# Low parts of the first pass's weights: from GpSimd halves to single VectorE operations

## The chip, the cores and the metric

The kernel runs on one core of one Trainium2 chip. That core has a matrix engine (TensorE, PE in the profile; its weight loads are PEld), a vector engine (VectorE, DVE), an activation engine (ScalarE, ACT), a general engine (GpSimd, POOL) and a queue that issues the transfers (SyncE, SP). The metric is the device time of one launch in microseconds (us), lower is better. Times from the profile belong to one profiled execution.

## The reference, cut to what matters

One decoder layer is computed in float32 for a prompt of 2048 rows and for 8 sample rows, with a model width of 1024. Nearly all of the work is products of an activation block with a weight matrix:

```python
h = rmsnorm(x, g_pre)
proj = h @ w_in                      # 1024 x 10248: q,k | v | o | z_a | gates | u | vb | z_b | merge gates
...                                  # conv + SiLU, mLSTM over 128-row chunks, chunk MLP
merged = jax.nn.sigmoid(gate_a) * (y_a @ w_pa) + jax.nn.sigmoid(gate_b) * (y_b @ w_pb)
x = x + rmsnorm(merged @ w_out, g_post)
x = x + jax.nn.sigmoid(x @ w_ple_gate) * rmsnorm(p @ w_ple, g_ple)
```

## The kernel before, in words

**Passes and units.** The prompt is cut into four passes of 512 rows (`p` = 0 to 3; the sample rows ride along in pass 1). In each pass the weights go by as 28 units of 512 columns, in the order of `PASS`: four heads with `v`, `qk`, `og`, `gg` each, then four `ub`, and two each of `pa`, `pb`, `wo` and `wg`. A unit is one block product with seven sub-products instead of eight (a Strassen-Winograd form): its weight is cut into A11, A12, A21, A22 of 512 rows by 256 columns, of which the sums S3 = A11 - A21, S2 = A22 - S3, S1 = A11 + S2 and S4 = A12 - S2 are made, and `ORDER` lists the seven weights that are multiplied: A11, A12, S2, S3, S1, A22, S4. Four passes of 28 units make 784 sub-products, 196 in each pass.

**High and low parts.** Each weight is a tile of 128 partitions by 1024 elements. It is split into a high part in the reduced format float32r (`whi`, a copy on ScalarE) and a low part (`wlo`, the weight minus its high part, made by `sub_hi`, line 129). A sub-product is 24 matmuls: high times high, high weight times low activation, low weight times high activation. So TensorE needs `wlo` in the third matmul of a sub-product.

**The stream of weights.** The class `Stream` prepares the weights some items ahead of the sub-product that runs (`run_unit`): `reach_high` makes the high part two items ahead and issues loads five items ahead (seven after the first pass), `reach_low` makes the low parts of what has a high part, and then, in the first pass, the sums up to three items ahead. In the first pass everything is made from the four loaded blocks; S3 is stored to memory as it is, and S2, S1 and S4 as high and low parts. In passes 1 to 3, S2, S1 and S4 come back already split, and four low parts per unit are made, all on VectorE.

**GpSimd's share.** In the first pass a counter, `uncut`, sends every fourth low part (items 3, 7, 11, ... of the 196, that is 49 of them) to GpSimd, as two subtractions of 128x512. The other 147 are made on VectorE, in one subtraction of 128x1024. As 196 items are seven per unit, the weight that goes to GpSimd changes from unit to unit: S3 in `v`, A11 and S1 in `qk`, A12 and A22 in `og`, S2 and S4 in `gg`, and so on.

**What sets the order.** Each engine works through its own list in order. The lists are fixed when the program is built: the framework's scheduler takes the instructions in the order of the code as priorities and places each on its engine by its own estimate of when operands and buffers are there; waits between engines are semaphores. The weight tiles (raw, sum, high, low) share 13 buffers (`wp`), so a tile that is used longer holds back a later one. GpSimd has other work of its own in all passes: the product of two gates (line 790), the chunk MLP's product (line 1293), the post-norm weight (line 1571), a merge addition (line 139), small copies for the convolution (lines 713 and 720) and the powers of the norms (lines 241 and 242). All transfers are issued from SP's queue.

Of the kernel before, what the change touches and what calls it, by code (L numbers as in the profile page):

```python
# [65 lines left out]
def order(unit):  # L66
    return LATE if unit == ("wo", 0) else ORDER


def width(unit):  # L70
    return 260 if unit == FIRST else 256
# [3 lines left out]
def tile_layer(ctx: ExitStack, tc: tile.TileContext, I, O):  # L75
    nc = tc.nc
    V, S, G, T = nc.vector, nc.scalar, nc.gpsimd, nc.tensor
# [35 lines left out]
    def spill(shape, name):  # L113
        return dp.tile(list(shape), F32, tag=name, name=name)
# [4 lines left out]
    def store(out, in_):  # L119
        nc.sync.dma_start(out=out, in_=in_)  # L120
# [7 lines left out]
    def sub_hi(eng, lo, full, hi):  # L128
        eng.tensor_tensor(lo, full, hi.bitcast(F32), op=ALU.subtract)  # L129
# [126 lines left out]
    class Stream:  # L256
# [4 lines left out]
        def __init__(self):  # L261
            self.items = [(p, u, n) for p in range(NP) for u in PASS for n, *_ in order(u)]
            self.loaded = self.summed = self.split = self.taken = 0
            self.raw, self.high, self.ready, self.kept = {}, {}, {}, {}
            self.uncut = 0

        def tile(self, u, name, dt=F32):
            return wp.tile([P, 4, width(u)], dt, tag="w", name=name)
# [68 lines left out]
        def reach_low(self, n):  # L337
            for key in list(self.high):
                hi = self.high.pop(key)
                lo = self.tile(key[1], "wlo", F32R)  # L340
                pool = key[0] == 0 and self.uncut % 4 == 3
                self.uncut += 1
                for k in ((slice(0, 2), slice(2, 4)) if pool else (slice(0, 4),)):
                    sub_hi(G if pool else V, lo[:, k], self.raw[key][:, k], hi[:, k])
                self.ready[key] = hi, lo
                _, u, name = key
                if name in CUT_KEPT:
                    self.kept[u, name] = [spill([P, 4 * width(u)], f"{name}{x}_{u[0]}{u[1]}") for x in "hl"]
                    for d, t in zip(self.kept[u, name], (hi, lo)):
                        store(d.rearrange("p (k c) -> p k c", k=4), t.bitcast(F32))  # L350
            while self.summed < min(len(self.items), n + self.SUM):
                self.sum(*self.items[self.summed])
                self.summed += 1
# [1406 lines left out]
```

## Time and profile before

| what | value |
|---|---|
| three runs | 2886.32 us median (2886.23 to 2891.51) |
| profiled execution | 2878.66 us, span 2877.0 us |
| granted TensorE clock, mean | 0.973 of full speed |
| PE, DVE, ACT, POOL busy | 94%, 75%, 54%, 18% of the span |
| memory traffic | 267 GB/s over the span |

The span is the time from the first to the last instruction. Busy time is the union of an engine's instructions. "Idle before" is the time that an engine stood still just ahead of a group of instructions, put down to what it waited for last. The first pass lies in the first 797 us: GpSimd's last low part ends at 796.9 us.

### The profile page before, as it was taken

Reading aid. Unit: us, or ns where it says so; the run is one execution under the profiler, and the core shown is the slowest. Engines: PE = TensorE matmul, PEld = TensorE weight load, DVE = VectorE, ACT = ScalarE, POOL = GpSimd, SP = SyncE. Lnnn points to the kernel's source line nnn. Section 1 sums busy time; section 2 is a strip of 40 time slices with the busy share of each in tenths; the row PEclk is TensorE's granted clock in tenths of the full one; section 3 lists DMA queues with packets and bytes.
Section 4 is the critical chain, followed back from the end, with each engine's and each line's share of the span. In section 5 each row is a group of like instructions: output and inputs, shape, how many; then the busy total and the mean of one; then the engine's idle time right before and its main releaser. Section 6 shows DMA issues by size and latency. Waiting matters only on the chain. (4 is left out here: it accounts for less than half of the span.)

```text
span 2877.0 us, 56022 instructions
## 1 busy us (share of the span) xinstructions
PE 2703.2 (94%) x21835; PEld 2639.0 (92%) x21835; DVE 2143.5 (75%) x3513; ACT 1540.1 (54%) x2668; POOL 512.8 (18%) x557
## 2 busy tenths in 40 slices
PE   6999999888899999999999999999999999999998
PEld 6899989888789899989889999999998999999898
DVE  8888888888977667766868766567678766665767
ACT  5555646445645555544456655564356545554445
POOL 3333332334310000101020100101111010101110
PEclk9999999899999999999999999999999999999999
DMA  6567667867777888889878777779878787788886
GB/s 223 220 249 273 242 235 267 295 253 255 262 257 249 287 267 273 276 272 328 285 250 294 254 260 257 253 258 322 311 277 298 241 268 262 252 272 279 317 283 231
DMA packets 268628, 770.37 MB, mean 268 GB/s; under 512 B 30066, under 2 KB 89338, under 8 KB 268355
## 3 DMA queue, kind: packets, MB, share of 16 engines
q1 hardware_dynamic: 268362, 766.79, 77.0%
q8 instruction: 172, 2.82, 0.4%
q14 instruction: 94, 0.76, 0.1%
HBM read 595.29 MB, written 171.53 MB: 267 GB/s over the span
## 5 line engine op out<-in xcount | busy, mean ns | idle before, releaser
L493 PE MATMUL acc<-rhi,whi 128*128 128x256 f32 (+1 forms) x4480 | 1289.6, 288 | 30.9 <-ACT s L124 8.9
L493 PE MATMUL acc<-rhi,wlo 128*128 128x256 f32 (+1 forms) x4480 | 1276.5, 286 | 43.1 <-DVE wlo L129 34.1
L493 PE MATMUL acc<-rlo,whi 128*128 128x256 f32 (+1 forms) x4480 | 1275.2, 285 | 0.0
L493 PEld LDWEIGHTS acc<-rhi,wlo 128*128 128x128 f32 x4480 | 859.3, 192 | 50.3 <-DVE wlo L129 39.6
L493 PEld LDWEIGHTS acc<-rhi,whi 128*128 128x128 f32 x4480 | 860.2, 192 | 41.6 <-ACT s L124 10.3
L493 PEld LDWEIGHTS acc<-rlo,whi 128*128 128x128 f32 x4480 | 859.4, 192 | 0.0
L129 DVE TENSOR_TENSOR wlo<-wraw,whi 128x1024 fp32r<-128x1024 f32 (+1 forms) x462 | 597.7, 1297 | 179.2 <-PE acc L493 77.2
L124 ACT ACTIVATE whi<-wraw 128x1024 fp32r<-128x1024 f32 (+1 forms) x504 | 530.1, 1055 | 349.6 <-PE acc L493 209.4
L490 PE MATMUL acc<-whi,rhi 128*128 128x256 f32 (+1 forms) x1792 | 517.7, 290 | 20.7 <-ACT rhi L124 6.7
L490 PE MATMUL acc<-wlo,rhi 128*128 128x256 f32 (+1 forms) x1792 | 512.0, 287 | 16.2 <-DVE wlo L129 14.1
L490 PE MATMUL acc<-whi,rlo 128*128 128x256 f32 (+1 forms) x1792 | 511.8, 286 | 6.3 <-DVE rlo L129 6.2
L490 PEld LDWEIGHTS acc<-whi,rhi 128*128 128x128 f32 x1792 | 346.1, 193 | 28.0 <-ACT rhi L124 9.6
L490 PEld LDWEIGHTS acc<-wlo,rhi 128*128 128x128 f32 x1792 | 345.1, 193 | 19.8 <-DVE wlo L129 16.9
L490 PEld LDWEIGHTS acc<-whi,rlo 128*128 128x128 f32 x1792 | 346.3, 193 | 8.2 <-DVE rlo L129 8.2
L124 ACT ACTIVATE u<-acc 128x512 f32<-128x512 f32 (+1 forms) x272 | 138.9, 517 | 209.8 <-PE acc L493 156.8
L129 POOL TENSOR_TENSOR wlo<-wraw,whi 128x512 fp32r<-128x512 f32 (+1 forms) x84 | 149.0, 1794 | 291.6 <-ACT whi L124 209.5
L124 ACT ACTIVATE s<-acc 128x512 f32<-128x512 f32 (+1 forms) x136 | 69.4, 513 | 79.3 <-PE acc L493 47.2
L790 POOL TENSOR_TENSOR so<-so,sz 128x512 f32<-128x512 f32 (+1 forms) x32 | 60.2, 1880 | 289.7 <-ACT so L774 171.9
L1293 POOL TENSOR_TENSOR yb<-yb,ub 128x512 f32<-128x512 f32 (+1 forms) x32 | 57.1, 1799 | 293.8 <-DVE ub L1291 127.0
L241 POOL TENSOR_SCALAR aab<-au 128x2 f32<-128x2 f32 x32 | 8.5, 266 | 481.6 <-DVE au L883 481.6
L869 DVE SCALAR_TENSOR_TENSOR cext<-cext,fst,smp 128x258 f32<-128x258 f32 x128 | 60.5, 479 | 36.1 <-PE smp L806 36.0
L720 POOL COPY halo<-raw 128x3 f32<-128x3 f32 x64 | 27.5, 454 | 284.8 <-DVE raw L139 154.7
(365 smaller groups left out, 3899.0 us busy)
## 6 DMA issues: line engine op xcount, KB each, us to landing
wraw<-in_w_main SPq DMA_DIRECT2D x351, 512.0 KB
xh<-xh SPq DMA_DIRECT2D x32, 512.0 KB
sg<-sgm SPq DMA_DIRECT2D x24, 512.0 KB
gsig<-sg SPq DMA_DIRECT2D x24, 512.0 KB
x<-in_x_prompt SPq DMA_DIRECT2D x16, 512.0 KB
ya<-ya SPq DMA_DIRECT2D x32, 256.0 KB
xr<-in_x_prompt SPq DMA_DIRECT2D x32, 256.0 KB
pg<-pg SPq DMA_DIRECT2D x32, 256.0 KB
```

Source lines behind the costliest of these rows:

```text
L124: S.activation(out, in_, AF.Copy)
L129: eng.tensor_tensor(lo, full, hi.bitcast(F32), op=ALU.subtract)
L241: G.tensor_scalar(out, ms, EPS, None, op0=ALU.add)
L490: T.matmul(outs[s], x[:, kt, s * P:(s + 1) * P], wt[:, kt, :], start=first, stop=last, skip_group_check=not opens)
L493: T.matmul(outs[s], wt[:, kt, s * P:(s + 1) * P], x[:, kt, :], start=first, stop=last, skip_group_check=not opens)
L720: G.tensor_copy(halo[:, ct, :], x[:, TP:TP + 3])
L790: G.tensor_tensor(so[:, s], so[:, s], sz[:, s], op=ALU.mult)
L869: V.scalar_tensor_tensor(cext[:, h, kt, :], cext[:, h, kt, :], gt.fst[:, h, self.c:self.c + 1], p3, op0=ALU.mult, op1=ALU.add)
L1293: G.tensor_tensor(y[:, :, l, :], y[:, :, l, :], ub[:, :, l, :], op=ALU.mult)
```

## The change

In the first pass the low part of every weight is now formed on VectorE, in one subtraction over the whole tile, as it was already done for three weights out of four and in the later passes. The counter goes. Nothing else in the code changes: the same operands, the same buffers, the same stores.

```diff
@@ class Stream, __init__
-            self.uncut = 0
@@ class Stream, reach_low
                 hi = self.high.pop(key)
                 lo = self.tile(key[1], "wlo", F32R)
-                pool = key[0] == 0 and self.uncut % 4 == 3
-                self.uncut += 1
-                for k in ((slice(0, 2), slice(2, 4)) if pool else (slice(0, 4),)):
-                    sub_hi(G if pool else V, lo[:, k], self.raw[key][:, k], hi[:, k])
+                sub_hi(V, lo, self.raw[key], hi)
                 self.ready[key] = hi, lo
```

## Rows read from the trace of the kernel before

**Rows 1.** The page: busy time, share of the span and instructions by engine.
```profile
PE 2703.2 (94%) x21835; PEld 2639.0 (92%) x21835; DVE 2143.5 (75%) x3513; ACT 1540.1 (54%) x2668; POOL 512.8 (18%) x557
```

**Rows 2.** Windows: stretch, its length, busy time (instructions) by engine, clock, transfers.
```profile
300.00:400.00 100.00, 93.55 (x752) 91.73 (x751) 86.08 (x128) 58.15 (x93) 34.08 (x34) 0.97 0.69 252
...
500.00:600.00 100.00, 82.68 (x606) 80.66 (x606) 83.30 (x81) 44.74 (x57) 32.97 (x18) 0.86 0.79 282
600.00:700.00 100.00, 83.45 (x617) 80.33 (x616) 93.39 (x97) 49.98 (x77) 44.38 (x19) 0.90 0.68 244
700.00:797.00 97.00, 80.50 (x635) 77.06 (x633) 83.00 (x117) 63.30 (x130) 39.94 (x32) 0.96 0.79 274
797.00:2877.00 2080.00, 2007.25 (x16444) 1963.22 (x16444) 1454.42 (x2604) 1095.82 (x1956) 226.03 (x324) 0.99 0.80 274
```

**Rows 3.** The tile wlo up to 797 us: count, least/median/longest ns.
```profile
L129 DVE TENSOR_TENSOR wlo<-wraw,whi x126: 1187/1218/2348, 16.0 to 788.9; 128x1024 fp32r<-128x1024 f32 x121, 128x1040 fp32r<-128x1040 f32 x5
L129 POOL TENSOR_TENSOR wlo<-wraw,whi x84: 1265/1728/7078, 22.7 to 794.6; 128x512 fp32r<-128x512 f32 x82, 128x520 fp32r<-128x520 f32 x2
...
L129 POOL TENSOR_TENSOR wlo<-wsum,whi x14: 1467/1732/2266, 112.1 to 778.4; 128x512 fp32r<-128x512 f32 x14
```

**Rows 4.** Waits of PE up to 797 us: us in total, times, longest.
```profile
PE acc L493 <- DVE wlo L129: 15.9, 10, 3.8
...
PE acc L493 <- POOL wlo L129: 8.8, 8, 1.9
PE acc L490 <- DVE wlo L129: 7.9, 7, 2.3
...
PE acc L490 <- POOL wlo L129: 2.1, 3, 1.0
```

**Rows 5.** Waits of DVE up to 797 us.
```profile
DVE wraw L136 <- POOL wlo L129: 8.1, 4, 2.4
...
DVE wlo L129 <- ACT whi L124: 2.0, 6, 0.6
```

**Rows 6.** DVE groups up to 797 us: count, busy us, mean ns, idle before.
```profile
L129 DVE TENSOR_TENSOR wlo<-wraw,whi 128x1024 fp32r<-128x1024 f32 x121 | 164.8, 1373 | 2.3 <-ACT whi L124 1.3 <-POOL wlo L129 0.6
L136 DVE TENSOR_TENSOR wraw<-wraw 128x1024 f32<-128x1024 f32 x27 | 40.0, 1482 | 26.3 <-DMA wraw<-in_w_main 22.7 <-DMA gple<-in_g_ple 3.5
...
L718 DVE SCALAR_TENSOR_TENSOR k<-raw,vecs,k 128x512 f32<-128x512 f32 x24 | 24.7, 1047 | 0.0
...
L129 DVE TENSOR_TENSOR cl<-cext,ch 128x516 fp32r<-128x516 f32 x16 | 15.1, 941 | 2.2 <-ACT ch L124 2.2
```

**Rows 7.** The same DVE groups after 797 us.
```profile
L718 DVE SCALAR_TENSOR_TENSOR k<-raw,vecs,k 128x512 f32<-128x512 f32 x72 | 51.2, 747 | 0.2
...
L129 DVE TENSOR_TENSOR cl<-cext,ch 128x516 fp32r<-128x516 f32 x48 | 33.3, 694 | 20.2 <-ACT ch L124 11.9 <-DMA wraw<-in_w_main 7.6 <-DMA out_C_sample<-cs 0.3
```

**Rows 8.** Timelines of DVE, POOL, ACT and PE: start, length, [idle before].
```profile
315.62 1.69 DVE L787 SCALAR_TENSOR_TENSOR sz<-sz,vecs,szg 128x512 f32<-128x512 f32 x1
317.23 2.28 DVE L129 TENSOR_TENSOR wlo<-wraw,whi 128x1024 fp32r<-128x1024 f32 x1
...
316.72 3.94 POOL L129 TENSOR_TENSOR wlo<-wsum,whi 128x512 fp32r<-128x512 f32 x2
...
312.43 1.07 ACT L124 ACTIVATE whi<-wsum 128x1024 fp32r<-128x1024 f32 x1 [1.18 <-DVE wsum L136]
...
318.48 0.39 PE L493 MATMUL acc<-rhi,wlo 128*128 128x256 f32 x1 [1.94 <-POOL wlo L129]
```

**Rows 9.** Window just behind that wait: columns as in rows 2.
```profile
320.00:323.40 3.40, 2.92 (x14) 2.69 (x13) 1.74 (x2) 2.25 (x4) 2.96 (x4) 0.50 0.59 182
```

**Rows 10.** Timelines of DVE and POOL near 610 us.
```profile
610.15 1.21 DVE L129 TENSOR_TENSOR wlo<-wraw,whi 128x1024 fp32r<-128x1024 f32 x1
...
609.39 5.48 POOL L129 TENSOR_TENSOR wlo<-wraw,whi 128x512 fp32r<-128x512 f32 x2 [11.14 <-ACT whi L124]
```

**Rows 11.** DVE groups from 500 to 797 us: columns as in rows 6.
```profile
L129 DVE TENSOR_TENSOR wlo<-wraw,whi 128x1024 fp32r<-128x1024 f32 x44 | 62.3, 1428 | 1.2 <-ACT whi L124 0.6 <-POOL wlo L129 0.6
```

## The prediction, made before the changed kernel had run

> **What bounds the kernel now.** I read the page's busy times first, then the stretches, then the waits inside the first pass. TensorE is busy for 94% of the span and VectorE for 75% [rows 1]. By stretch the two lie closer together. After 797 us TensorE is busy for 2007 of 2080 us, 96.5% [rows 2]: passes 1 to 3 have little left that another engine could give back, and the change does not touch their code. In a head of the first pass (300 to 400 us) TensorE is busy for 93.6 and VectorE for 86.1 of 100 us. In the later part of the first pass (500 to 797 us) TensorE falls to 246.6 of 297 us, VectorE rises to 93.4 of 100 us in one of the stretches, and the granted clock is 0.86 to 0.96 [rows 2]. So the bound is TensorE, and what the change can move is its idle time in the first pass, with VectorE as the engine that stands nearest behind it.
>
> The waits say what that idle time is made of. Up to 797 us the matmuls wait 15.9 + 7.9 = 23.8 us for low parts from VectorE and 8.8 + 2.1 = 10.9 us for low parts from GpSimd [rows 4]. GpSimd makes one in four, and costs about a third of the wait.
>
> **What is removed.** 98 halves go from GpSimd, with medians of 1.73 us [rows 3]: a low part takes it 2 x 1.73 = 3.5 us. Nothing on GpSimd waits behind that on the path, so its 175 us of time are worth nothing by themselves. What counts is that TensorE waits for their ends, 10.9 us, and that VectorE waits 8.1 us before sums that must not overwrite a weight still being read by GpSimd [rows 5]. The second is idle time of an engine with some to spare, and I count it as nothing.
>
> One such wait in detail: in each of three heads TensorE stands 1.94 us for the low part of an S2. Its high part was there at 312.43 + 1.07 = 313.50 us, but GpSimd, in order, reached it at 316.72 and needed 3.94 us for both halves [rows 8]. On VectorE the same low part can't start before 313.50; if the two VectorE operations around that time stay ahead of it, it ends near 316.8 instead of 320.66. So most of this wait goes and a few tenths stay. I count 9 of the 10.9 us as saved; the bounds are 10.9 and nothing.
>
> **What is added.** 49 subtractions of 128x1024 on VectorE, with a median of 1.22 us [rows 3]: 59.8 us. Up to 797 us VectorE is idle for about 108 us in all (the stretches of [rows 2] and the four like them before), so they would fit, but would raise it from 86% to 94%. SP's queue gets the same transfers; the stores of low parts wait for their makers as before.
>
> **What is given back on VectorE.** This term decides the sign. Where GpSimd works on a half, VectorE's own operations are stretched: a subtraction that takes 1.22 us takes 2.28 us beside GpSimd's half at 316.72 [rows 8], and its longest is 2.35 us [rows 3]. The groups show the sum. The largest group's mean is 1373 ns against the 1218 of the median: 121 x 155 = 18.8 us. The sums on line 136: 27 x (1482 - 1218) = 7.1 us. The convolution taps on k take 1047 ns here and 747 later, 24 x 300 = 7.2 us, and the low part of the state 941 against 694, 16 x 247 = 4.0 us [rows 6, 7]. These four come to 37 us; a dozen smaller groups of the same view, taken in the same way, bring it to 61 us. Not all of it is the low parts' doing, as GpSimd multiplies gates and branches in the same stretch. Bounds: 37 us, if only these four groups get shorter, and 61 us. Most of GpSimd's operations on two tiles in this pass are these halves, so I take 55 us. VectorE's work then changes by 59.8 - 55 = about +5 us in 797, between -1 and +23. That is hidden by its idle time; without that cover it would be 5 us on the path.
>
> **Waits for VectorE's own low parts (23.8 us).** Two things pull on them. Fewer operations are stretched to twice their length just when TensorE wants their result, and 49 more stand in an in-order list. A low part that waits for its high part holds up everything behind it on VectorE: the sums, the evacuations of results, the state updates. The nearest row: the low parts that are made there now waited 2.0 us in all for high parts [rows 5], 147 of them, so 49 more would add 0.7 us. I take the two as equal, with 12 us of gain (half the wait) and 21 us of loss (17 low parts after 500 us at 1.22 us, nothing given back there) as ends.
>
> **The clock.** Right behind the wait at 316 to 320 us the granted clock is 0.50 for 3.4 us [rows 9], the lower of the two levels (1.2 GHz); before it TensorE had stood for 1.94 us and 0.5 us. At half clock 3.4 us hold 1.7 us of full-speed work. A second such stretch lies behind a wait for GpSimd near 645 us. Two of them: 3 us of gain if the waits are gone, nothing if others come in their place.
>
> **The sum.** -9 for GpSimd's low parts, 0 for VectorE's, -3 for the clock, 0 for the rest: -12 us. The profiled execution took 2878.66 us, of which 2877.0 is the span and 1.7 lies around it; it would become 2867. It ran 7.7 us below the median of the three runs, 2886.32 us, and it is the median that a new kernel is held against, so I carry the difference over: 2874 us.
>
> **The rivals.**
>
> *No change (2886 us).* TensorE stops waiting for GpSimd and waits as long for VectorE, because the longer list delivers other things later. For it: TensorE already waits more than twice as long for VectorE's low parts as for GpSimd's [rows 4], and VectorE is at 93.4 of 100 us in one stretch [rows 2]. Against it: in the heads VectorE has 14 us of 100 free. In this case belongs also that the change does not do what it says: GpSimd's other products keep stretching VectorE's operations, so that little is given back, while TensorE's waits become shorter.
>
> *Slower (2898 us).* In the merge and output part, after 500 us, VectorE is the engine that holds on, and GpSimd the one that is held. Then VectorE loses nothing there now, and gets 17 x 1.22 = 21 us more work in stretches where it has 16.7, 6.6 and 14 us free. For it: near 610 us GpSimd needs 5.48 us for two halves while VectorE's subtraction beside it takes its plain 1.21 us [rows 10], and one half took 7.08 us [rows 3]. Against it: the 44 low parts that VectorE makes after 500 us have a mean of 1428 ns, so it does lose, 44 x 210 ns = 9 us on these alone [rows 11]. If two thirds of the 21 us reached TensorE, 14 us, with 4 us more of lowered clock and 6 us of gain kept in the heads, the time is 2886 + 12 = 2898 us. It decides itself at 600 to 700 us: if VectorE goes from 93 to 98 of 100 us there, this case holds. The Trainium skill speaks for it in two places: in "SBUF — State Buffer", section "Who interferes with whom", a VectorE operation with two SBUF inputs and a GpSimd operation that reads SBUF exclude each other, and whichever starts second is blocked until the other ends; an engine whose list is full would mostly be first. And "Perfetto Trace Analysis", section "Optimizing Scalar/DVE Operations", holds that with VectorE saturated it may make sense to offload to ScalarE or even GpSimd, with the warning that the shared port may eat the gain. By these the stretch after 500 us should lose the full 21 us, 2907 us less the heads' gain of 6, 2901 us; the trace bears it out in single places only.
>
> *Larger gain (2856 us).* The stretched operations are what makes TensorE wait for VectorE in the later part. Then half of the 23.8 us goes with them, and the clock, 0.86 and 0.90 in two stretches [rows 2], gains some 6 us more: -12 - 12 - 6 = -30 us. For it: the waits and the stretched operations lie in the same places. Against it: the added 49 operations lie there too.
>
> **How the numbers follow.** The likeliest case, a gain of some 12 us, gets 0.43, the larger gain 0.12, no change 0.24, slower 0.21. What a measurement of this kernel can tell is about 0.2%, 5.8 us: faster is below 2880.5, slower above 2892.1. The first two cases give faster 0.55, the third the same 0.24, the last slower 0.21. The range takes in most of the larger gain and of the slower case: 2855 to 2898 us. The likeliest case alone, with GpSimd's waits saved between half and all and the clock or not, is 2870 to 2881.
>
> **What would show it.** Right: no GpSimd operation on `wlo`; VectorE's low parts near 1.22 to 1.27 us on average in the first pass and its busy time up to 797 us within some 10 us of now; TensorE's waits for low parts of the first pass under 28 us in all (34.7 now); the first pass's end near 785 us; passes 1 to 3 as long as now. Wrong: VectorE's busy time 30 us or more higher (nothing given back); waits for VectorE's low parts that grew by the 10.9 us that went; a later part with VectorE full; or passes 1 to 3 that change by more than some 5 us, since the lists are planned anew when the program is built and none of the above counts that.

## The result and the profile after

The changed kernel takes 2844.43 us (median of 4 runs, 2833.46 to 2850.03) against 2886.78 us before: a ratio of 0.9857, 95% interval 0.9836 to 0.9878. That is 42 us less, three and a half times the 12 us of the forecast, and under the lower end of the range (2855 us). The direction was right, the size was not. The profiled execution took 2833.46 us.

The page and the stretches of the changed kernel first (the removed lines shift its numbers: L489 and L486 are L493 and L490 of before). Columns of the stretches as in [rows 2].

```profile
PE 2678.7 (95%) x21835; PEld 2615.1 (92%) x21835; DVE 2141.3 (76%) x3562; ACT 1541.6 (54%) x2668; POOL 339.2 (12%) x459
```
```profile
17.70:757.00 739.30, 671.49 (x5373) 652.70 (x5372) 680.26 (x947) 431.86 (x688) 106.47 (x108) 0.97 0.74 266
757.00:2831.70 2074.70, 2000.13 (x16435) 1955.76 (x16433) 1453.90 (x2601) 1096.20 (x1956) 224.88 (x323) 0.99 0.80 274
```
The first pass of the kernel before, from its first matmul of a weight to its end:

```profile
17.70:797.00 779.30, 689.24 (x5359) 669.65 (x5359) 681.81 (x895) 430.71 (x688) 280.09 (x211) 0.94 0.70 252
```

The first pass went from 779.3 to 739.3 us, 40 us. (Its end before is taken at 797 us as in [rows 2]; the first weight matmul of the next pass stands at 798.2 us before and at 757.0 us after, which makes it 41 us.) The later passes went from 2080 [rows 2] to 2074.7 us. That is within what they vary by: in the profiles of the runs below that touch the first pass alone they take between 2072 and 2085 us. VectorE makes 49 more low parts, yet its busy time in the first pass is 680.3 us where it was 681.8. TensorE's 40 us fall into two parts: it stands idle for 739.3 - 671.5 = 67.8 us instead of 90.1, and the same matmuls keep it busy for 17.8 us less, as the granted clock is 0.97 instead of 0.94.

The low parts, the waits and VectorE's groups up to 757 us, against [rows 3 to 6]:

```profile
L129 DVE TENSOR_TENSOR wlo<-wraw,whi x168: 1185/1216/2340, 16.2 to 752.6; 128x1024 fp32r<-128x1024 f32 x162, 128x1040 fp32r<-128x1040 f32 x6
L129 DVE TENSOR_TENSOR wlo<-wsum,whi x28: 1207/1217/2336, 24.9 to 737.1; 128x1024 fp32r<-128x1024 f32 x27, 128x1040 fp32r<-128x1040 f32 x1
```
```profile
PE acc L489 <- DVE wlo L129: 19.3, 19, 4.0
PE acc L486 <- DVE wlo L129: 10.5, 9, 2.5
...
DVE wlo L129 <- ACT whi L124: 7.9, 12, 3.1
```
```profile
L129 DVE TENSOR_TENSOR wlo<-wraw,whi 128x1024 fp32r<-128x1024 f32 x162 | 200.3, 1246 | 8.0 <-ACT whi L124 7.9
...
L136 DVE TENSOR_TENSOR wraw<-wraw 128x1024 f32<-128x1024 f32 x27 | 33.5, 1243 | 10.3 <-DMA wraw<-in_w_main 10.3
...
L714 DVE SCALAR_TENSOR_TENSOR k<-raw,vecs,k 128x512 f32<-128x512 f32 x24 | 17.3, 743 | 0.0
...
L865 DVE SCALAR_TENSOR_TENSOR cext<-cext,fst,smp 128x258 f32<-128x258 f32 x32 | 14.9, 475 | 0.8 <-PE smp L802 0.6
L129 DVE TENSOR_TENSOR cl<-cext,ch 128x516 fp32r<-128x516 f32 x16 | 13.2, 825 | 0.9 <-ACT ch L124 0.9
```

The low part of a loaded weight takes 1246 ns on average instead of 1373, the taps on k 743 instead of 1047, the low part of the state 825 instead of 941. The waits for low parts are 19.3 + 10.5 = 29.8 us, where they were 34.7 for both makers together: that is 4.9 us of the 22.3 us of idle time. Most of the rest lies in waits for other things that VectorE delivers, which the forecast had left out:

```profile
PE acc L493 <- DVE sz L139: 7.4, 4, 2.1
...
PE smp L806 <- DVE cl L129: 4.1, 3, 1.7
PE smp L806 <- DVE ql L129: 3.1, 2, 2.5
```

These rows are of the kernel before, up to 797 us; after, `sz` comes to 1 us and the other two are not in the list. Together 13 us. (`sz` is the gate that VectorE takes out of a result of TensorE; `cl` and `ql` are low parts of the state and of q.) The wait of the heads that [rows 8] showed looks like this after the change (timelines of VectorE, ScalarE, GpSimd and TensorE):

```profile
303.09 1.22 DVE L129 TENSOR_TENSOR wlo<-wsum,whi 128x1024 fp32r<-128x1024 f32 x1
...
301.49 1.05 ACT L124 ACTIVATE whi<-wsum 128x1024 fp32r<-128x1024 f32 x1
...
301.45 5.16 POOL L786 TENSOR_TENSOR so<-so,sz 128x512 f32<-128x512 f32 x1 [24.20 <-DVE sz L783]
...
304.36 0.39 PE L489 MATMUL acc<-rhi,wlo 128*128 128x256 f32 x1 [0.33 <-DVE wlo L129]
```

The low part of S2 follows its high part by 0.55 us and is done at 304.31. TensorE waits 0.33 us for it, where it waited 1.94: a few tenths stay, as the prediction had it. GpSimd's gate product takes 5.16 us here, beside a busy VectorE: it is GpSimd that is late, and TensorE does not wait for it.

### The profile page after: what moved, and what is told of

Same layout as the page of the kernel before. It is cut to its first block, busy times and chain, and to the rows that moved or that the text cites. A ratio compares the mean times of both kernels' runs of the same rounds, so it can differ in the third digit from the quotient of the medians.

```text
span 2831.7 us, 55890 instructions
## 1 busy us (share of the span) xinstructions
PE 2678.7 (95%) x21835; PEld 2615.1 (92%) x21835; DVE 2141.3 (76%) x3562; ACT 1541.6 (54%) x2668; POOL 339.2 (12%) x459
## 4 chain that ended last, share of the span: by engine, by line
PE 56%; DVE 8%; DMA 5%; ACT 2%; issue 2%; POOL 1%; SPq 0%; DVEq 0%; ACTq 0%; POOLq 0%
PE acc L489 34%; PE acc L486 14%; PE smp L802 3%; DVE wlo L129 2%; DVE rlo L129 1%; PE smp L495 1%; DMA blk<-yb 1%; DMA cs<-in_state_C 1%; PE smp L822 1%; PE smp L1187 1%; PE smp L1264 1%; DMA xh<-xh 0%; SPq L117 0%; ACT rhi L124 0%; ACT whi L124 0%
## 5 line engine op out<-in xcount | busy, mean ns | idle before, releaser
L489 PE MATMUL acc<-rhi,whi 128*128 128x256 f32 (+1 forms) x4480 | 1281.2, 286 | 26.6 <-ACT u L124 11.1
L489 PE MATMUL acc<-rhi,wlo 128*128 128x256 f32 (+1 forms) x4480 | 1267.4, 284 | 38.2 <-DVE wlo L129 38.0
L489 PE MATMUL acc<-rlo,whi 128*128 128x256 f32 (+1 forms) x4480 | 1266.8, 283 | 0.0
L489 PEld LDWEIGHTS acc<-rhi,wlo 128*128 128x128 f32 x4480 | 849.6, 190 | 46.8 <-DVE wlo L129 46.3
L489 PEld LDWEIGHTS acc<-rhi,whi 128*128 128x128 f32 x4480 | 851.2, 190 | 37.6 <-ACT u L124 13.6
L489 PEld LDWEIGHTS acc<-rlo,whi 128*128 128x128 f32 x4480 | 850.3, 190 | 0.0
L129 DVE TENSOR_TENSOR wlo<-wraw,whi 128x1024 fp32r<-128x1024 f32 (+1 forms) x504 | 634.5, 1262 | 183.9 <-PE acc L489 72.3
L486 PE MATMUL acc<-whi,rhi 128*128 128x256 f32 (+1 forms) x1792 | 516.6, 289 | 19.5 <-ACT rhi L124 6.3
L486 PE MATMUL acc<-wlo,rhi 128*128 128x256 f32 (+1 forms) x1792 | 510.9, 287 | 15.8 <-DVE wlo L129 15.7
L486 PE MATMUL acc<-whi,rlo 128*128 128x256 f32 (+1 forms) x1792 | 510.7, 286 | 5.8 <-DVE rlo L129 5.8
L486 PEld LDWEIGHTS acc<-whi,rhi 128*128 128x128 f32 x1792 | 345.3, 193 | 25.6 <-ACT s L124 7.4
L486 PEld LDWEIGHTS acc<-wlo,rhi 128*128 128x128 f32 x1792 | 344.1, 193 | 19.1 <-DVE wlo L129 19.1
L486 PEld LDWEIGHTS acc<-whi,rlo 128*128 128x128 f32 x1792 | 345.6, 193 | 7.5 <-DVE rlo L129 7.4
L129 DVE TENSOR_TENSOR rlo<-blk,rhi 128x1024 fp32r<-128x1024 f32 (+1 forms) x48 | 62.7, 1312 | 20.6 <-ACT rhi L124 20.3
L714 DVE SCALAR_TENSOR_TENSOR q<-raw,vecs,q 128x512 f32<-128x512 f32 x96 | 66.6, 747 | 4.1 <-ACT q L710 4.1
```

Of the source, the lines that this page charges most:

```text
L486: T.matmul(outs[s], x[:, kt, s * P:(s + 1) * P], wt[:, kt, :], start=first, stop=last, skip_group_check=not opens)
L489: T.matmul(outs[s], wt[:, kt, s * P:(s + 1) * P], x[:, kt, :], start=first, stop=last, skip_group_check=not opens)
L714: V.scalar_tensor_tensor(o, x[:, j:j + TP], convw[:, j, ct:ct + 1], o, op0=ALU.mult, op1=ALU.add)
```

## The experiments

All were measured beside the kernel before (2886 to 2888 us); a ratio is to that. Two theories stood at the start: A, that GpSimd's subtractions stretch VectorE's operations and TensorE stalls on those; B, that TensorE waited for GpSimd's late halves. A third, C: the engines' lists are planned anew at build time, and the new ones may be better by themselves. In the traces before and after, 308 of VectorE's 3513 operations do not stand in the same order, and TensorE's list differs too.

**The changed kernel once more**, with blank lines for the removed ones:

> The changed kernel once more, with blank lines in place of the removed ones so that line numbers are those of before. Contention, latency and order theories all expect 2840 to 2850 us (ratio 0.985 to 0.987); it is the yardstick for the others of this call.

Measured: 2843.76 us, 0.9864 (0.9838 to 0.9891).

**Contention alone.** The low parts as after the change; GpSimd does work that nobody needs, in 45 pairs of subtractions (`dout` is a tile of 128x480 that is idle in this pass; the lines that count and that make it are left out):

```diff
+                ...
+                for k in (0, 512) if self.uncut % 4 == 0 and self.uncut < 183 else ():
+                    x = hi.bitcast(F32).rearrange("p a b -> p (a b)")[:, k:k + 480]
+                    G.tensor_tensor(dout, x, x, op=ALU.subtract)
```

> All low parts on VectorE as in the changed kernel; beside every fourth, GpSimd makes two subtractions of 128x480 of the high part into a tile that nobody reads (45 pairs, until the last units of the first pass). The lists of TensorE, ScalarE and VectorE are those of the changed kernel; nobody waits for GpSimd. Theory A (GpSimd's halves stretch VectorE's operations, and that makes TensorE stall and its clock fall): VectorE's operations stretch by some 55 us again on top of the 60 us that it now has, VectorE is nearly full in the first pass, and the time is 2890 us or more. Rival B (TensorE waited for GpSimd's late low parts, and little else): nobody waits for these, so 2845 us, within 8. Rival C (the new lists of instructions, planned anew, are better by themselves): also 2845 us.

Measured: 2884.11 us, 1.0001 (0.9988 to 1.0014). The whole gain is gone although no engine waits for these subtractions and the lists of TensorE and ScalarE are the same (VectorE's too, but for one operation). B alone and C alone fall; A holds, a little under its 2890 us. Its stretch of the first pass, its groups and its waits:

```profile
17.80:805.00 787.20, 689.73 (x5374) 668.28 (x5373) 725.86 (x948) 432.54 (x690) 257.19 (x203) 0.95 0.70 250
```
```profile
L129 DVE TENSOR_TENSOR wlo<-wraw,whi 128x1024 fp32r<-128x1024 f32 x162 | 212.9, 1323 | 11.6 <-ACT whi L124 11.6
...
L718 DVE SCALAR_TENSOR_TENSOR k<-raw,vecs,k 128x512 f32<-128x512 f32 x24 | 21.6, 925 | 0.0
...
L869 DVE SCALAR_TENSOR_TENSOR cext<-cext,fst,smp 128x258 f32<-128x258 f32 x32 | 14.9, 476 | 1.4 <-PE smp L806 1.3
...
L344 POOL TENSOR_TENSOR slhs<-whi 128x480 f32<-128x480 f32 x90 | 148.4, 1649 | 310.2 <-ACT whi L124 307.1
```
```profile
PE acc L493 <- DVE wlo L129: 32.5, 26, 4.2
...
PE acc L490 <- DVE wlo L129: 10.5, 8, 4.0
```

VectorE is busy for 45.6 us more than in the changed kernel with the same instructions, and TensorE waits 43 us for its low parts instead of 30. This run has both the 49 low parts and the stretching on VectorE, which neither kernel had together, so it bounds what the stretching costs; it does not measure its share in the kernel before. The state update `cext`, which reads one of its two tiles from PSUM, stays at 476 ns (475 after the change). It is so for all groups of four and more operations that read a tile of PSUM: 122 us in sum in both runs, while the other groups go from 584 to 629 us.

**GpSimd writes only.** Instead of the subtraction, a one-element memset on VectorE and `G.memset(dout, 0.0)` twice:

> As the run with GpSimd's idle subtractions, but GpSimd only writes zeros (two memsets of 128x480 in the same places, released by a one-element memset on VectorE ahead of each). Theory A in the form that it is GpSimd's reading that holds VectorE up: 2845 to 2855 us (the 90 one-element memsets cost VectorE some 5 to 10 us of its slack). If any GpSimd operation on a tile holds VectorE up: near the time of the run with the subtractions, 2870 us or more.

Measured: 2845.30 us, 0.9859 (0.9833 to 0.9885).

```profile
L344 POOL MEMSET slhs<- 128x480 f32 x90 | 45.0, 499 | 166.2 <-DVE slhs L344 162.7 <-DVE mc L652 3.2
```
```profile
L129 DVE TENSOR_TENSOR wlo<-wraw,whi 128x1024 fp32r<-128x1024 f32 x162 | 199.9, 1245 | 7.3 <-ACT whi L124 6.7 <-ACT num L126 0.6
...
L718 DVE SCALAR_TENSOR_TENSOR k<-raw,vecs,k 128x512 f32<-128x512 f32 x24 | 17.4, 752 | 0.0
```

VectorE's groups are as long as in the changed kernel, and its busy time in the first pass is 681.6 us where it was 680.3. A GpSimd operation that only writes costs VectorE nothing that can be seen here; the memsets are shorter than the subtractions, 45 us in all against 148. VectorE even stood still for 17.1 us, up to 1.3 us at a time, until GpSimd's memset had ended, before its own memsets; that cost no time that shows, so a hold costs by where it falls. This is what the Trainium skill states in "SBUF — State Buffer", section "Who interferes with whom": a VectorE operation with two SBUF inputs is in conflict with a GpSimd operation that reads SBUF, and not with one that only writes it; with at most one SBUF input, outside of some faster modes, it is in conflict with neither. The traces agree in all three points: 1323 against 1246 ns beside reads, 1245 beside writes, 476 against 475 with one input in PSUM.

**All but the seven that TensorE waited for**, and **only those seven** on GpSimd:

```diff
-                pool = key[0] == 0 and self.uncut % 4 == 3
+                pool = key[0] == 0 and self.uncut % 4 == 3 and self.uncut not in (51, 79, 107, 163, 171, 179, 195)
+                pool = key[0] == 0 and self.uncut in (51, 79, 107, 163, 171, 179, 195)   # the other run
```

> As before the change, GpSimd makes every fourth low part in halves, but not the seven for which TensorE was seen to wait (items 51, 79, 107, 163, 171, 179, 195 of the first pass): 42 of 49 stay on GpSimd. Theory A: nearly all of the stretching stays, so 2876 us or more (a gain of at most 10 us over before). Rival B: nearly all of the gain comes, 2845 to 2855 us. Rival C says nothing sure.

Measured: 2861.72 us, 0.9915 (0.9885 to 0.9945): between the two. 42 low parts for which hardly anybody waits cost 18 us over the changed kernel; TensorE waits 7.4 us for `sz` again, and not for GpSimd:

```profile
PE acc L493 <- DVE sz L139: 7.4, 4, 2.1
...
PE acc L493 <- POOL wlo L129: 0.3, 1, 0.3
```

> The complement of the run before: only the seven low parts for which TensorE was seen to wait (items 51, 79, 107, 163, 171, 179, 195) are made by GpSimd in halves, the other 42 on VectorE. If the two costs add up (waits for late halves 24 us, as the run without them gained; stretching by the other 42 some 18 us): 2844 + 24 = 2868 us, within 6. If the waits were only where stretching shows up (theory A alone: 7 of 49 of the contention, 7/49 x 42 = 6 us): 2850 us.

Measured: 2854.78 us, 0.9889 (0.9865 to 0.9914). Seven low parts cost 11 us, and TensorE waits for them:

```profile
PE acc L493 <- POOL wlo L129: 12.3, 5, 4.5
...
PE acc L490 <- POOL wlo L129: 1.2, 2, 0.7
```

So both theories have a share: 11 us for the seven that are late (with what little they stretch) and 18 us for 42 that are hardly waited for. All executions of both runs lie above all of the changed kernel, but by the intervals each of the two losses is known only to some 10 us. Together the 49 cost 42 us, and the two losses add up to 29; neither expectation for the seven (2868 and 2850 us) was met.

**Stage by stage**: GpSimd's share in the heads only (`self.uncut < 112`), or only behind them (`>= 112`).

> GpSimd makes every fourth low part in the 16 units of the heads (28 of 49), VectorE the rest. By the lengths of the stages in the two traces (heads 422.8 us before and 400.3 after, the rest 357.7 and 338.9) the heads' share of the gain is 22 us and the rest's 19: 2866 us. If the loss sat in the dense later part of the first pass (the slower rival's place, in reverse): 2850 us.

> GpSimd makes every fourth low part in the ub, pa, pb, wo and wg units of the first pass (21 of 49), VectorE those of the heads. By the same shares 2844 + 19 = 2863 us; if the gain sat in the heads alone, 2846 us.

Measured: 2865.65 us, 0.9927 (0.9902 to 0.9952), and 2861.78 us, 0.9921 (0.9901 to 0.9941). Losses of 22 and 18 us, 40 in sum, as expected: by stage the costs add up within the noise, and the dense later part of the first pass gains as the heads do.

**The rest of GpSimd's work on two tiles as well on VectorE** (lines 790, 1293, 1571 and 139 called with `V` instead of `G`), on top of the change, then without it:

> The changed kernel, and GpSimd's other products and additions on two tiles (the gates' product, the chunk MLP's product, the post-norm weight, the merge's addition: 112 operations in four passes, 1.5 to 2.0 us each) also on VectorE, where one takes 0.68 us. By the rule of contention (given back about what is added) VectorE's busy time stays within 20 us of the changed kernel's 2141 us; as these products wait for nothing late, TensorE gains little: 2838 us, between 2828 and 2848. If VectorE's list becomes the limit in the dense stretches: 2850 us or more.

Measured: 2821.92 us, 0.9775 (0.9737 to 0.9813), 22 us under the changed kernel, the best but one here, and below the expected 2828 to 2848. Between the two profiles 5 us of it lie in the first pass (739.2 to 734.1 us) and 13 in the later ones (2074.7 to 2061.8). The page, and the low parts up to 830 us:

```profile
PE 2675.7 (95%) x21835; PEld 2613.9 (93%) x21835; DVE 2155.5 (77%) x3666; ACT 1545.8 (55%) x2668; POOL 159.2 (6%) x355
```
```profile
L129 DVE TENSOR_TENSOR wlo<-wraw,whi x182: 1185/1222/1247, 16.2 to 826.0; 128x1024 fp32r<-128x1024 f32 x172, 128x1040 fp32r<-128x1040 f32 x10
```

104 more recorded operations on VectorE, of 0.68 us each, 71 us, raise its busy time by 14 us. The longest low part of a loaded weight is now 1.25 us; in the changed kernel some took 2.34.

> The other half of the run with everything on VectorE: low parts as before the change (every fourth on GpSimd in halves), but the gates' product, the chunk MLP's product, the post-norm weight and the merge's addition on VectorE. If the two moves add up (that run lay 22 us under the changed kernel): 2887 - 22 = 2865 us, within 7. If GpSimd, freed of them, delivers its low parts so much earlier that the waits for them go as well (the products stood ahead of the S2 low parts in its list): 2855 us or less.

Measured: 2848.02 us, 0.9864 (0.9843 to 0.9884). The low parts are on GpSimd as before the change, and yet 38 us are gained, nearly as much as the change itself gained. The time is that of the second expectation; its reason, that the waits for GpSimd's low parts go, is not what happened:

```profile
PE acc L493 <- POOL wlo L129: 6.3, 8, 1.3
...
PE acc L490 <- POOL wlo L129: 1.7, 1, 1.7
```

These waits fell from 10.9 to 8.0 us only. The first pass got 13 us shorter, the later ones 18 in sum (by the first weight matmul of each pass, 2078.7 to 2061.0 us). GpSimd makes no low parts there, so most of this gain is another one than that of the change. It fits that GpSimd's other products held VectorE up in those passes; no run tells that from their being late themselves.

**Every second low part on GpSimd** (`% 2 == 1`), and **each in one piece** (`(slice(0, 4),)` for both engines):

> GpSimd makes every second low part of the first pass in halves (98 of 196, twice as many as before). By the dose so far (0: 2844, 49: 2887 us) a straight line gives 2929 us, and late halves that queue behind one another more: 2930 to 2950. If VectorE's relief began to outweigh (its own 98 low parts less), 2890 us or less.

Measured: 2908.09 us, 1.0081 (1.0060 to 1.0102): slower, by half of the straight line. Of the wait rows `sz` is the one that grew most (7.4 to 17.0 us):

```profile
PE acc L493 <- DVE wlo L129: 20.6, 10, 8.8
PE acc L493 <- DVE sz L139: 17.0, 4, 4.5
```

> As before the change, but GpSimd makes its 49 low parts in one subtraction of 128x1024 each. The total that VectorE loses stays about the same 60 us by theory A, but a single hold is up to 2.5 us instead of 1.3, and TensorE gets the low part in one step: 2890 to 2905 us. If the fixed cost of a second GpSimd operation was what hurt: 2875 us.

Measured: 2891.83 us, 1.0029 (1.0013 to 1.0044), as expected. Halves were the better form, by 5 us. A single hold is longer (VectorE's longest low part takes 3.43 us, 2.35 before), and TensorE's waits for GpSimd's low parts double, to 21.6 us from 10.9; no run tells the two apart:

```profile
PE acc L493 <- POOL wlo L129: 17.7, 7, 4.6
...
PE acc L490 <- POOL wlo L129: 3.9, 2, 3.0
```
```profile
L129 DVE TENSOR_TENSOR wlo<-wraw,whi x128: 1186/1216/3433, 16.0 to 824.7; 128x1024 fp32r<-128x1024 f32 x121, 128x1040 fp32r<-128x1040 f32 x7
L129 POOL TENSOR_TENSOR wlo<-wraw,whi x42: 2345/2574/8156, 22.6 to 807.3; 128x1024 fp32r<-128x1024 f32 x41, 128x1040 fp32r<-128x1040 f32 x1
```

**The small copies too**, on ScalarE, on top of everything on VectorE:

> The run with everything on VectorE, and the 128 small copies of the convolution (128x3, 0.3 to 0.9 us on GpSimd) on ScalarE as well. They hold VectorE up little, as they are short: 2822 us within 5. If they do hold it up at each of 128 places for 0.3 us, 2800 us; if ScalarE's list delays TensorE, 2830 us or more.

Measured: 2819.73 us, 0.9763 (0.9736 to 0.9790). As expected, it can't be told from the run without it; both beat both kernels.

## Why the prediction was wrong in size, step by step

**What bounds it: right.** TensorE, and its idle time in the first pass. 40 of the 45 us between the profiles lie there.

**Removed, 9 of 10.9 us: right.** GpSimd's low parts are waited for no longer, and of the wait worked out in detail 0.33 us stayed. More than half of it came back as waits for VectorE's low parts, 29.8 us where 23.8 were.

**Added and given back: right, at the end of its bounds.** 59.8 us were added, and VectorE's busy time in the first pass fell by 1.5 us, so 61.3 us were given back, where 55 were taken and 61 was the upper bound. The sign, the step that was said to decide, was right. The "slower" rival, that VectorE holds on in the dense part, fell: with GpSimd's low parts left in that part alone 18 us are lost, and from 600 to 700 us VectorE is busy for 90.6 of 100 us, where 93.4 were and 98 was the sign.

**Waits for VectorE, 0 with ends of -12 and +21: the first step that failed.** It counted only the low parts of weights. Their waits rose by 6.0 us. What VectorE delivers besides (`sz`, `cl`, `ql`) stood under "0 for the rest" without a reason, and 13 us of waits for these went. They were in the same view as [rows 4]. A hold of one or two us hits whatever stands behind it in VectorE's list, so the waits to go through are those for everything that the stretched engine makes. With VectorE's busy time unchanged, the idle time of TensorE fell by 22.3 us, where -9 was the sum of the two terms.

**The clock, 3 us: the second step, and nearly as large.** It counted two lowered stretches that stand behind waits for GpSimd (ahead of the second, near 645 us, TensorE had also waited 1.36 us for ScalarE). But in the profile the same matmuls keep TensorE busy for 17.8 us less. From 67 to 510 us, where the heads lie, the kernel before has five stretches of 3.4 us at 0.50, the lower level of 1.2 GHz. One is that of [rows 9]; these are the other four. They stand behind waits for VectorE: at 205.85, 305.99 and 407.64 us TensorE had waited 2.1, 2.1 and 2.0 us for `sz`, at 465.84 us 2.5 us for `ql`. (The clock is the third figure from the end.)

```profile
207.30:210.70 3.40, 3.40 (x18) 3.40 (x18) 3.40 (x5) 0.74 (x2) 0.00 (x0) 0.50 0.38 147
306.30:309.70 3.40, 3.40 (x18) 3.40 (x17) 3.40 (x5) 0.64 (x1) 0.00 (x0) 0.50 0.02 5
...
408.70:412.10 3.40, 3.40 (x19) 3.40 (x18) 3.40 (x5) 0.56 (x2) 0.00 (x0) 0.50 0.24 96
466.70:470.10 3.40, 3.40 (x19) 3.40 (x18) 3.31 (x5) 1.43 (x4) 0.00 (x0) 0.50 0.00 1
```

The changed kernel has none there:

```profile
67.00:510.00 443.00, 424.24 (x3511) 416.24 (x3509) 407.13 (x593) 272.59 (x425) 60.80 (x73) 1.00 0.74 269
```

Not every wait was followed by one: behind the waits of 1.93 and 1.94 us for GpSimd's S2 in two other heads the clock stayed at 1.00. These stretches of the changed kernel answer to [rows 2]; as the work moved forward in time, they do not hold quite the same matmuls:

```profile
300.00:400.00 100.00, 96.34 (x799) 94.71 (x798) 93.89 (x141) 64.15 (x100) 18.09 (x20) 1.00 0.73 262
500.00:600.00 100.00, 81.44 (x615) 77.88 (x614) 91.25 (x95) 46.99 (x56) 9.15 (x5) 0.93 0.82 293
600.00:700.00 100.00, 84.75 (x660) 81.68 (x658) 90.55 (x113) 56.58 (x124) 19.42 (x13) 0.95 0.71 256
```

The head at 300 us is at full clock throughout (0.97 before), 500 to 600 us at 0.93 (0.86), 600 to 700 us at 0.95 (0.90). Where the waits of the heads went, the lowered clock behind them went as well, and most of these waits were for VectorE. That shorter waits raised the clock is read from these rows; no run changed the clock alone. Its size also differs from one execution to the next: the four runs of the changed kernel have mean clocks of 0.976 to 0.985 and times of 2850 to 2833 us, in that order at the ends. So the share of the clock in the 42 us of the medians is known only roughly.

**The larger gain (2856 us), a chance of 0.12,** came nearest: stretched operations make TensorE wait for VectorE, and the clock adds to it. But the wait it named, half of the 23.8 us for VectorE's low parts, did not go; those waits rose, others went instead, most of them in the heads and not in the later part, and the gain was 12 us larger. No change fell because the longer list did not deliver other things later: the waits for `sz`, `cl` and `ql` are what shrank.

**The signs.** VectorE's low parts (1.25 us on average over both groups), its busy time and the missing GpSimd operations came as said. TensorE's waits for low parts are 29.8 us where under 28 was the sign, the first pass ends at 757 us and not near 785, and the later passes changed by the 5 us that were allowed.

**What stays open.** How the 42 us split between lateness and stretching: the two losses, 11 and 18 us when each stands alone, add up to 29 us, and the gap of 13 us is hardly more than the noise of the four medians that it is worked out from. Also open is what the new order of the lists adds or takes. The contention-only run shows that the changed kernel's lists alone do not bring the gain, not that they have no part in it.

## What to carry to other kernels

Work that is moved to GpSimd to relieve VectorE must be priced with what it takes from VectorE: compare the means of VectorE's operations beside it and away from it, add the differences up, and hold the sum against the time that the work would take on VectorE (here 61 against 60 us, so the move had bought nothing). Then count all waits of the bounding engine for the stretched one, not only those for the moved operation, and look for lowered clock behind each. Here the sum was even, and with all low parts on VectorE the kernel was faster.

## What was not expected of the hardware

Moving the low parts and the four kinds of products and additions from GpSimd, 161 operations in four passes, changed VectorE's busy time by 12 us in 2143 while GpSimd's fell from 513 to 159 us. The same held with GpSimd's share at 98 low parts (2147 us). In this kernel VectorE's busy time was nearly the same on whichever of the two engines this work was done; what changed was how long TensorE waited. And one GpSimd operation beside a full VectorE could take four times as long as the quickest of its kind (5.16 us against 1.29 for the gates' product in the changed kernel): either engine can be the one that is held.
